# The last output projection with seven block products (Strassen) for each pair of token tiles in place of eight

## The chip, the core and the metric

The kernel runs on one core of one Trainium2 chip. A core has five engines that work side by side, each on its own queue in order: TensorE (PE in the profile, its weight loads PEld), VectorE (DVE), ScalarE (ACT), GpSimd (POOL) and SyncE (SP), which here only issues DMAs. ACT issues DMAs too. TensorE writes its results to PSUM, eight banks of 512 f32 columns; the other data lie in SBUF, 128 partitions wide. The metric is the device time of one execution in microseconds, lower is better. The kernel before takes 1339.58 us (median of 3 runs, 1339.54 to 1339.79).

## The reference

The program is one step of a two-layer backbone: a gated linear attention (GLA) layer, then a grouped-query attention layer, on 256 context tokens and 1024 latent tokens with 1024 features. What the change touches is the last line of the second layer:

```python
out_p = (attend_blocks(qp, kp, vp) * jax.nn.silu(gp)) @ att_w_out[i]
...
out_s = (attend_blocks(qs, keys, vals) * jax.nn.silu(gs)) @ att_w_out[i]
xp = xp + gt_p * out_p
xs = xs + gt_s * out_s
```

So 1280 rows of 1024 gated values are multiplied by a 1024 x 1024 matrix, scaled column by column with a gate vector and added to the residual. All of it is f32.

## The kernel before

**Precision.** TensorE is fed with f16. Each f32 matrix is scaled by a power of two and split into a high part (the f16 rounding) and a low part (the rest, again f16). A product is three matmuls: high x high, high x low, low x high (`mm3`, L120, which is why most matmuls have line 125). The high part is made by ACT, the low part by VectorE with a scalar-tensor-tensor operation that reads the f32 source and the high part. The scale comes from a maximum (VectorE), a small matmul that spreads it over the partitions (`pow2`, L79, the matmul is L84) and a chain of small VectorE operations.

**Stages.** After the start (the modulation vectors, the first normalisation) comes the GLA loop (`gla`, L642) with 50 slots, one for a head and a token tile. In a slot TensorE does projections, the scan's matmuls and whatever `filler` adds: the later weights are loaded, scaled and split here in jobs. `split_ahead` (L189) does that for the second layer's weights, 256 columns a job: load into a `wst` buffer (there are two), four maxima, the scale, four high parts (L203), four low parts (L204), and four DMAs to DRAM. `AHEAD` names the slots; the four jobs for `att_w_out` (names `o0`, `o1`) are the last ones, at slots 25 to 31. The scan's state passes through GpSimd (L571), as do a sum of two masked matrices (L537) and other small operations.

After the GLA's output projection the attention (`attention`, L1057) runs ten steps of four heads. For each head and pair of token tiles: scores (L974) into an S tile of three PSUM banks (there are two S tiles), the maximum (L977), the exponential (L982), the split of the probabilities by GpSimd (L1003) and VectorE (L1004), and a transposing DMA into `PT` (L1005). Two heads later `values` (L1018) multiplies `PT` with the values, 30 matmuls of 256 columns, and writes the gated result to `og2_d` in DRAM. `gateT` (L1008) makes the gate from `hT_hi` and `hT_lo`, the normalised activations; the last `gateT` is the last reader of these two tiles. In steps 6 and 9 the split output weights come back from DRAM into the `wtile` places 2 and 1 (`wload`, with the DMAs handed out one a head through `later`).

**The last projection.** Token tiles are taken in pairs in the order `OUT = (1, 0, 2, 3, 4)`. `out2_load` (L1103) brings the pair's 256 rows back, transposed, into `wst`; `out2_prep` (L1108) takes two maxima (L1113), the scale, two high parts (L1120) and two low parts (L1121), each of 1024 columns. `out_tile` (L1126) does one token tile: `residual` (L715) multiplies it with 512 columns of the weights at a time, 24 matmuls for a bank of an S tile, then VectorE scales (L723) and adds the residual row (L724) and ACT issues the store (L726). The first pair's operands are made in the attention's last step, in the place of the rotary table (`ropet`), and its first token tile stands ahead of the last two `values`; the rest is in `att_out` (L1135). The last tile is cut into 512, 256 and 256 columns.

**Order.** The program is written for a scheduler that tracks which instruction needs which, simulates the engines' times when the kernel is built and fixes the order on each engine by that; `issue_after` holds a block behind a given instruction. The order on the chip is therefore near to the program's order, but not the same: loads are issued where their buffer comes free, and two token tiles' matmuls alternate.

## Time and profile before

| | |
|---|---|
| median of the runs | 1339.58 us |
| the profiled execution, first to last instruction | 1339.8 us |
| granted TensorE clock, mean | 0.980 |
| TensorE busy | 1240.6 us (93%) |
| VectorE busy | 928.7 us (69%) |
| ScalarE busy | 662.8 us (49%) |
| GpSimd busy | 402.0 us (30%) |
| first matmul of the last projection | 1220.48 us |
| last matmul of it | issued and done by 1336.04 us |

The page gives busy time by engine over the whole span. The windows give the same for a stretch. The chain that ended last is followed back from the last instruction, at each step to what released it; in order of time it reads as "start, duration, what". A group row reads: line, engine, operation, output <- inputs, shapes, count | total busy us, mean ns of one | idle time ahead of it and what ended it. A row of one line's view gives minimum, median and maximum instead of a mean. All in all 22669 instructions are recorded.

### The profile page before, as it was taken

To read this page: it belongs to the slowest core of one execution; us is meant where nothing else is said; L and a number is where in the kernel's file an instruction comes from. 1 tells how busy PE (TensorE), PEld (TensorE's weight loads), DVE (VectorE), ACT (ScalarE), POOL (GpSimd) and SP (SyncE) were. 2 spreads that over 40 slices of the span, in tenths; PEclk is the share of its full clock that TensorE was granted. 3 is DMA by queue.
4 is the path that set the end of the run, shared out by engine and by line. 5 is a ranking of instruction groups with operands and counts; after the bars stand their busy time and mean duration, and the time that the engine had idled before them with its cause. 6 is when DMAs were issued, how large, how long until landed. Compare 5 with 4: busy or idle time off the path is not lost. (4 is left out here: it accounts for less than half of the span.)

```text
span 1339.8 us, 22669 instructions
## 1 busy us (share of the span) xinstructions
PE 1240.6 (93%) x8150; PEld 808.5 (60%) x8150; DVE 928.7 (69%) x2138; ACT 662.8 (49%) x1661; POOL 402.0 (30%) x623
## 2 busy tenths in 40 slices
PE   4789999999999999698899998999988998989998
PEld 2357765655555556475677656767665766766444
DVE  1876868886868688756564567878567687877552
ACT  2565546655646566533333455555556565553110
POOL 1232213322322133401222435544333343523000
PEclk9899999999999999898999999999989999999999
DMA  9612455544545532357552278877938748788532
GB/s 306 226 63 93 145 181 182 160 150 155 185 134 170 174 114 83 96 166 227 142 150 101 66 201 140 144 138 131 197 72 169 147 80 150 173 150 195 179 134 79
DMA packets 344770, 199.15 MB, mean 149 GB/s; under 512 B 229406, under 2 KB 331534, under 8 KB 343376
## 3 DMA queue, kind: packets, MB, share of 16 engines
q1 hardware_dynamic: 297024, 159.67, 47.5%
q10 hardware_dynamic: 47312, 37.25, 8.8%
q8 instruction: 64, 1.05, 0.3%
q0 software_dynamic: 320, 0.77, 0.2%
q14 instruction: 50, 0.41, 0.1%
HBM read 104.31 MB, written 37.24 MB: 106 GB/s over the span
## 5 line engine op out<-in xcount | busy, mean ns | idle before, releaser
L125 PEld LDWEIGHTS <-hT_hi 128*128 128x128 f16 x1440 | 142.5, 99 | 105.3 <-issue 9.6
L125 PE MATMUL mm<-whi,hT_hi 128*128 128x512 f16 (+1 forms) x560 | 196.6, 351 | 7.9 <-ACT gx L471 7.8
L125 PE MATMUL mm<-wlo,hT_hi 128*128 128x512 f16 (+1 forms) x560 | 196.4, 351 | 0.0
L125 PE MATMUL mm<-whi,hT_lo 128*128 128x512 f16 (+1 forms) x560 | 196.3, 351 | 0.0
L125 PEld LDWEIGHTS <-whi 128*128 128x128 f16 x1368 | 134.2, 98 | 76.2 <-issue 9.2
L1003 POOL TENSOR_SCALAR phl<-p,srec 128x1280 f16<-128x1280 f32 (+1 forms) x80 | 106.4, 1330 | 198.6 <-DVE srec L998 106.6
L125 PE MATMUL mm<-hT_hi,whi 128*128 128x256 f16 (+1 forms) x512 | 153.3, 302 | 4.3 <-POOL hT_hi L349 2.9
L125 PE MATMUL mm<-hT_lo,whi 128*128 128x256 f16 (+1 forms) x512 | 153.8, 301 | 0.2 <-DVE hT_lo L350 0.2
L125 PE MATMUL mm<-hT_hi,wlo 128*128 128x256 f16 (+1 forms) x512 | 153.8, 301 | 0.0
L1004 DVE SCALAR_TENSOR_TENSOR phl<-p,srec,phl 128x1280 f16<-128x1280 f32 (+1 forms) x80 | 107.5, 1344 | 54.0 <-POOL phl L1003 53.9
L125 PE MATMUL mm<-PT,vh 128*128 128x256 f16 x672 | 118.4, 281 | 20.2 <-DMA PT<-phl 13.5
L974 PE MATMUL S<-kT,wst 128*128 128x512 f16 (+1 forms) x624 | 122.1, 338 | 3.6 <-ACT p L982 3.6
L982 ACT ACTIVATE p<-S,snb,sexp 128x1280 f32<-128x1280 f32 (+1 forms) x80 | 99.6, 1245 | 19.4 <-DVE srec L998 9.7
L977 DVE TENSOR_REDUCE smx<-S 128x1 f32<-128x1280 f32 (+1 forms) x80 | 101.5, 1270 | 11.0 <-PE S L974 10.9
L125 PEld LDWEIGHTS <-hT_lo 128*128 128x128 f16 x720 | 71.2, 99 | 49.4 <-DVE hT_lo L350 0.5
L125 PE MATMUL mm<-PT,vl 128*128 128x256 f16 x336 | 94.5, 281 | 0.0
L974 PEld LDWEIGHTS <-wst 128*128 128x128 f16 x624 | 61.0, 98 | 55.1 <-issue 4.2
L125 PEld LDWEIGHTS <-wlo 128*128 128x128 f16 x720 | 70.6, 98 | 37.3 <-issue 1.6
L125 PEld LDWEIGHTS <-vh 128*128 128x128 f16 x672 | 66.9, 101 | 33.7 <-issue 15.0
L147 DVE TENSOR_REDUCE wmx<-wst 128x1 f32<-128x512 f32 x104 | 64.5, 676 | 23.7 <-DMA wst<-in_gla_w_in 9.8
L979 ACT ACTIVATE snb<-smx,nsexp 128x1 f32<-128x1 f32 x80 | 23.4, 293 | 110.7 <-DVE smx L977 105.0
L125 PE MATMUL y<-whi,ogT 128*128 128x256 f16 (+1 forms) x336 | 75.8, 316 | 2.6 <-DVE p2s L96 1.0
(335 smaller groups left out, 2705.2 us busy)
## 6 DMA issues: line engine op xcount, KB each, us to landing
wada<-in_w_ada SPq DMA_DIRECT2D x16, 1024.0 KB, 5.0
wst<-in_gla_w_in SPq DMA_DIRECT2D x12, 1024.0 KB, 5.7
wst<-in_att_w_in SPq DMA_DIRECT2D x10, 1024.0 KB, 8.4
xr<-x_d SPq DMA_DIRECT2D x11, 512.0 KB, 3.3
og_d<-gx ACTq DMA_DIRECT2D x40, 128.0 KB, 1.8
og_d<-og ACTq DMA_DIRECT2D x40, 128.0 KB, 3.0
wst<-og_d SPq DMA_DIRECT2D x5, 1024.0 KB
out<-xr ACTq DMA_DIRECT2D x17, 256.0 KB, 2.0
```

What stands on the lines that cost most here:

```text
L125: self.nc.tensor.matmul(out, a, b, start=k == 0 and j == 0, stop=k == n - 1 and j == 2)
L147: nc.vector.tensor_reduce(mx[:, j : j + 1], st[:, 2 * j : 2 * j + 2, :], AX.XY, ALU.max, apply_absolute_value=True)
L974: nc.tensor.matmul(S[:, a : a + n], x, y, start=m == 0, stop=m == 2)
L977: last = nc.vector.tensor_reduce(mx, S, AX.X, ALU.max).ins
L979: nc.scalar.activation(nb, mx, AF.Copy, scale=self.nsexp)
L982: nc.scalar.activation(p, S, AF.Exp, scale=self.sexp, bias=nb, accum_out=den)
L1003: nc.gpsimd.tensor_scalar(hi, p, r, 2.0 ** 14, ALU.mult, ALU.mult)
L1004: nc.vector.scalar_tensor_tensor(lo, p, r2, hi, ALU.mult, ALU.subtract)
```

## The change

The 2 x 2 block form of the product is used in Winograd's version of Strassen's method. For a pair of token tiles the left matrix is cut in two by tokens (128 each) and in two by the inner dimension (512 each), the weights in two by the inner dimension and in two by columns. Eight block products of 12 matmuls (4 inner steps x 3) become seven, of these operands: left a11, S2, S1, S3, a12 - S2 and so on (sums of quarters), right B11, T2, T1, T3, B22, T4, B21. The sums are formed in f32, then split into high and low parts; the scales leave room for a factor of four.

- *Weights.* `split_ahead` no longer handles `att_w_out`. `split_products` does, a generator with four parts that run in two slots, four times (slots 25 to 33): GpSimd scales four quarters in place, forms four differences and three of the low parts, ACT makes seven high parts, VectorE four low parts; seven DMAs go to `win_d`. Four of the seven weight blocks are loaded where `o0` and `o1` were; the other three go into `hT_hi` and `hT_lo` when these are free.
- *Operands.* `sums` and `sums_rest` make seven operands of 512 columns a pair (`cut`: high part on ACT, low part on VectorE), with four sums on GpSimd. Rows of odd pairs are loaded into a second place (`og1`, in `hT_lo`), so two loads can be on the way.
- *Products.* `pair_start` does the first four products, `pair_end` the other three, of which each accumulates onto an earlier product in its bank. Two copies by ACT, four additions by VectorE and one by GpSimd combine them. `store` scales (VectorE), adds the residual (two of four on VectorE, two on GpSimd; in the last pair three on VectorE) and issues the DMA. The fourth bank is the one of the pair's scale matmul (for the first pair, a bank of the other S tile). The last product of the last pair is cut into two halves of 256 columns.
- The first pair's `pair_start` stands ahead of the last two `values`, `pair_end` behind them.

```diff
+    def split_products(self, b, st):
+        s, inv = self.scale(st)
...
+        for x in (b11, b22, b12, b21):
+            nc.gpsimd.tensor_scalar(x, x, s4, 1.0, ALU.mult, ALU.mult)
+        def put(m, x):
...
+            nc.scalar.copy(hi, x)
+            (nc.gpsimd if m in (B11, B21, T4) else nc.vector).tensor_tensor(lo, x, hi, ALU.subtract)
+            nc.scalar.dma_start(self.win_d[:, m, :, b], t[0][:, (t[1] - 1) % 2])
+        sub = lambda o, x, y: nc.gpsimd.tensor_tensor(o, x, y, ALU.subtract)
+        put(B11, b11)
+        put(B22, b22)
+        sub(b11, b12, b11)
+        sub(b12, b22, b12)
+        sub(b22, b22, b11)
+        yield
+        put(T1, b11)
+        put(B21, b21)
+        yield
+        put(T3, b12)
+        put(T2, b22)
+        yield
+        sub(b21, b21, b22)
+        put(T4, b21)
+        yield
...
         self.rest()
+        self.out2_load(OUT[1], self.og1)
+        for j, (t, m) in enumerate(((self.hT_hi, 2), (self.hT_lo, 1))):
...
+                for part in range(2):
+                    self.nc.sync.dma_start(w[:, part], self.win_d[:, len(wo), part])
...
+        self.fold_gate(1, self.win_inv, gt)
...
+        pair = self.pair_start(OUT[0], ops, wo, x, scale, [tmp[:, 512 * j : 512 * j + 512] for j in range(3)])
...
+        self.sums_rest(row, ops, scale)
         for t in pend:
             self.values(*t, g.pop(t[0]))
+        self.pair_end(*pair)
...
+    def cut(self, x, s, to):
+        nc.scalar.activation(to[:, 0], x, AF.Copy, scale=s)
+        nc.vector.scalar_tensor_tensor(to[:, 1], x, s, to[:, 0], ALU.mult, ALU.subtract)
...
+    def sums(self, og, to, late=True):
...
+        ps = self.bank("mm") if late else None
+        s, inv = self.pow2(m, ps=ps)
+        a11, a12, a21, a22 = self.quarters(og)
+        g = nc.gpsimd.tensor_tensor
+        g(a21, a21, a22, ALU.add)
+        self.cut(a11, s, to[0])
+        g(a11, a21, a11, ALU.subtract)
+        self.cut(a21, s, to[2])
+        self.cut(a11, s, to[1])
+        g(a21, a22, a11, ALU.subtract)
+        self.cut(a21, s, to[3])
+        return s, inv, ps
+    def sums_rest(self, og, to, scale):
+        a11, a12, a21, a22 = self.quarters(og)
+        self.nc.gpsimd.tensor_tensor(a11, a12, a11, ALU.subtract)
+        self.cut(a11, scale[0], to[4])
+        self.cut(a22, scale[0], to[5])
+        self.cut(a12, scale[0], to[6])
+    def product(self, ps, x, w, start=True, b=0, n=4):
+        for k in range(4):
+            for j, (u, v) in enumerate(((0, 0), (0, 1), (1, 0))):
+                self.nc.tensor.matmul(
+                    ps[:, P * b : P * (b + n)], x[:, u, k], w[:, v, b : b + n, k],
...
+    def pair_start(self, c, ops, w, x, scale, tmp):
...
+        self.product(ps[0], ops[0], w[B11])
+        nc.scalar.copy(t1, ps[0])
+        self.product(ps[1], ops[1], w[T2])
+        self.product(ps[2], ops[2], w[T1])
+        nc.scalar.copy(t3, ps[2])
+        nc.vector.tensor_tensor(t2, ps[1], t1, ALU.add)
+        self.product(ps[3], ops[3], w[T3])
+        nc.gpsimd.tensor_tensor(t3, t3, t2, ALU.add)
+        nc.vector.tensor_tensor(t3, ps[3], t3, ALU.add)
+    def pair_end(self, c, ops, w, x, inv, u, v, ps, last=False):
...
+        store(1, 1, v)
+        self.product(ps[2], ops[4], w[B22], start=False)
+        nc.vector.tensor_tensor(ps[2], ps[2], u, ALU.add)
+        store(0, 1, ps[2], add=nc.vector)
+        self.product(ps[3], ops[5], w[T4], start=False)
+        nc.vector.tensor_tensor(u, ps[3], u, ALU.add)
+        store(1, 0, u, add=nc.vector if last else nc.gpsimd)
+        for b, n in ((0, 2), (2, 2)) if last else ((0, 4),):
+            self.product(ps[0], ops[6], w[B21], False, b, n)
+            store(0, 0, ps[0], b, n, nc.vector)
     def att_out(self, wo):
...
+        now = prep(1, self.og1)
+        og = get(2)
+        for n in range(1, 5):
+            later = get(n + 2)
+            nxt = prep(n + 1, og) if n < 4 else None
...
+            self.pair_end(*self.pair_start(c, ops, wo, x, scale, tmp), last=n == 4)
+            now, og = nxt, later
...
         def filler(slot):
+            n, m = divmod(slot - PRODUCTS, 2)
+            if 0 <= n <= 4 and (n, m) != (4, 1):
+                if m == 0:
+                    if n:
+                        next(rounds[0])
+                    if n < 4:
+                        rounds[:] = [k.split_products(n, k.stage_out(n))]
+                        k.jobs.append((next, rounds[0]))
+                else:
+                    next(rounds[0])
+                    k.jobs.append((next, rounds[0]))
```

More of the change, by code (lines that the diff above doesn't have):

```diff
@@ L44 @@
 OUT = (1, 0, 2, 3, 4)
+PRODUCTS = 25
+B11, T2, T1, T3, B22, T4, B21 = range(7)
 G_SCALE = 32.0
@@ L139, in stage, with stage_out @@
         self.nc.sync.dma_start(st, ap.rearrange("(k p) n -> p k n", p=P))
+        return st
+    def stage_out(self, b):
+        st = self.t(self.wst, [P, KT, 256], F32, "wst")
+        src = self.I["att_w_out"][0].rearrange("(k p) (x b n) -> p k x b n", p=P, x=2, b=4)
+        for x in range(2):
+            self.nc.sync.dma_start(st[:, :, P * x : P * x + P], src[:, :, x, b])
         return st
@@ L1091, in attention @@
                     first = self.ropet.rearrange("p a b d -> p (a b d)").bitcast(F16)
-                    first = first.rearrange("p (j h t) -> p j h t", j=2, h=AH)
+                    first = first.rearrange("p (m a k t) -> p m a k t", m=4, a=2, k=4)
                     with self.tc.issue_after(self.last):
-                        self.prep = self.out2_prep(row, (first[:, 0], first[:, 1]))
+                        ops = [first[:, m] for m in range(4)]
+                        scale = self.sums(row, ops, False)
@@ L1111, in out2_prep, with quarters @@
+    def quarters(self, og):
+        v = og.rearrange("p (x k) (r t) -> p r x k t", x=2, r=2)
+        return [v[:, r, x] for r in range(2) for x in range(2)]
+    def sums(self, og, to, late=True):
+        nc = self.nc
         mx = self.t(self.small, [P, 2], F32, "wmx")
@@ L1264, in emit @@
             cols += [(f"q{b}", W[:, 512 * b : 512 * b + 512]), (f"g{b}", W[:, g0 + 512 * b : g0 + 512 * b + 512])]
[L1265 removed]
         cols = [(n, j, w[:, 256 * j : 256 * j + 256]) for n, w in cols for j in range(2)]
         queue = [(0, b) for b in (8, 9, 10, 11)] + [(1, b) for b in (4, 5, 6, 7, 0, 1, 2, 3, 8, 9, 10, 11)]
[L1268 removed]
+        wo, part, prep, held, rounds = [], [], [], [], []
         def filler(slot):
```

117 lines of the change are left out of this document (75 added, 42 removed).

## The prediction

> **What bounds the kernel now.** I read the page's first part, then the chain that ended last, then the groups by line, then the windows around the two places that the diff touches. The page names one engine:
>
> ```profile
> PE 1240.6 (93%) x8150; PEld 808.5 (60%) x8150; DVE 928.7 (69%) x2138; ACT 662.8 (49%) x1661; POOL 402.0 (30%) x623
> ```
>
> The chain, in order of time, says how TensorE spends the last stage, in which the output projection runs. The first row is from the timeline: the first matmul of that stage.
>
> ```profile
> 1220.48 0.38 PE L125 MATMUL S<-whi,ropet 128*128 128x512 f16 x1
> ```
> ```profile
> 1230.95 0.70 DVE p L724
> 1231.65 0.04 issue
> ...
> 1237.04 3.38 PE mm L125 x31
> ...
> 1275.61 0.22 PE mm L84 x2
> ...
> 1291.60 36.27 PE S L125 x168
> 1327.87 0.03 issue
> 1327.89 0.77 DVE S L723
> 1328.66 0.02 issue
> 1328.69 0.70 DVE xr L724
> 1329.39 0.04 issue
> 1329.43 2.79 PE S L125 x24
> ...
> 1333.25 2.79 PE S L125 x24
> ...
> 1336.07 0.50 DVE S L723
> 1336.60 0.42 DVE xr L724
> ```
>
> One 128x512 matmul costs 36.27/168 = 0.216 us, one of 256 columns 2.79/24 = 0.116 us in this stage and 3.38/31 = 0.109 us in `values`. From 1220.48 to the end of the last matmul, 1336.04, are 115.6 us. The work in it is the equivalent of 480 x 0.216 = 103.6, two `values` of 30 matmuls (6.5) and four scale matmul pairs (0.9): 111.0. So 4.6 us are idle. What I read there: TensorE waits for VectorE's add on one bank of an S tile before it writes the next bank of the same S tile (1329.43 follows 1329.39, 1231.70 follows 1231.65). Where two token tiles alternate this is covered; in the last tile it isn't. After the last matmul 1339.8 - 1336.04 = 3.8 us are left (scaling, addition, store).
>
> **The change part by part.** The sum is made against the profiled span, 1339.8; the median of the runs, 1339.58, is 0.2 lower.
>
> *Removed on TensorE.* 5 pairs x 12 matmuls = 60 x 0.216 = -12.9 us, all of it on the path. The moving operand becomes four pieces of 128 columns, 512 elements apart; the decay matmul already reads two such pieces and costs what contiguous 256 columns cost (273 in the hT row further down), so I add nothing:
>
> ```profile
> L484 PE MATMUL z<-wa,r 98*128 98x256 f16 x40 | 11.0, 274 | 0.2 <-DVE g L493 0.2
> ```
>
> The 4.6 us idle also goes out of the sum and idle of the new order comes in. Base: 420 x 0.216 + 6.5 + 0.9 = 98.1; 1220.5 + 98.1 + 3.8 = 1322.4 without any wait.
>
> *(a) End of the last pair.* The last product is halved within one bank. After product six VectorE adds, scales and adds again (0.689 + 0.756 + 0.689, rows below, 2.2 with gaps); the first half takes 12 x 0.116 = 1.4, and its scaling and addition (0.50 + 0.42) come only after those. The second half starts 3.2 after product six: 1.8 us idle. The wait between banks of one S tile returns between products one and two (ACT's copy, 0.72): 0.9. Product four has its own bank and could cover it; between pairs the next pair covers it. Sum +2.7, bounds 1.8 to 1.8 + 5 x 0.9 = 6.3.
>
> *(b) VectorE and GpSimd in the pairs.*
>
> ```profile
> L204 DVE SCALAR_TENSOR_TENSOR split<-wst,p2s,split 128x512 f16<-128x512 f32 x56 | 40.8, 760 | 7.2 <-ACT split L203 7.1
> L203 ACT ACTIVATE split<-wst,p2s 128x512 f16<-128x512 f32 x56 | 37.4, 720 | 24.6 <-DVE p2s L96 18.1 <-DMA w_g<-split 3.1 <-DMA w_q<-split 1.9
> L723 DVE SCALAR_TENSOR_TENSOR S<-S,p2i,wst 128x512 f32<-128x512 f32 x19 | 14.4, 756 | 35.8 <-PE S L125 35.8
> L724 DVE TENSOR_TENSOR xr<-S,xr 128x512 f32<-128x512 f32 x17 | 11.7, 689 | 1.1 <-DMA xr<-x_d 0.8
> L1113 DVE TENSOR_REDUCE wmx<-wst 128x1 f32<-128x1024 f32 x10 | 11.7, 1210 | 5.8 <-DMA wst<-og_d 5.8
> L1121 DVE SCALAR_TENSOR_TENSOR wlo<-wst,p2s,whi 128x1024 f16<-128x1024 f32 x8 | 10.1, 1280 | 5.4 <-ACT whi L1120 5.4
> L88 DVE TENSOR_REDUCE p2m<-o 128x1 f32<-128x128 f32 x32 | 9.1, 283 | 3.1 <-PE o L84 2.8
> L96 DVE TENSOR_SCALAR p2s<-p2e 128x1 int32<-128x1 int32 x47 | 7.1, 150 | 1.0
> ```
>
> VectorE per pair, before: two maxima 2.4, scale chain 0.28 + 5 x 0.15 = 1.0, two low parts 2.6, four scalings and additions 5.8: 11.8 of 96 x 0.216 + 0.2 = 20.9. After: 2.4 + 1.0 + seven low parts of 512 (7 x 0.76 = 5.3) + four sums of products (2.8) + four scalings (3.0) + two additions (1.4) = 15.9 of 84 x 0.216 + 0.2 = 18.3, so 87%. ACT has 9 x 0.72 = 6.5 and is no bound. GpSimd, idle in this stage, gets seven 128x512 tensor-tensor operations. No row has that size; the shortest of two sizes give the slope:
>
> ```profile
> L835 POOL TENSOR_TENSOR rope<-hx,ropet x160: 307/320/1566, 647.5 to 1172.2; 128x64 f32<-128x64 f32 x160
> ```
> ```profile
> L537 POOL TENSOR_TENSOR at<-am x40: 450/534/867, 112.1 to 540.1; 128x128 f32<-128x128 f32 x40
> ```
>
> (450 - 307)/64 = 2.2 ns per element, so 1.3 us for 512 and 9.2 us per pair. The maxima of these rows are the warning, and the next three rows explain them:
>
> ```profile
> 1206.97 2.54 POOL L1003 TENSOR_SCALAR phl<-p,srec 128x1280 f16<-128x1280 f32 x1 [3.70 <-DVE srec L998]
> ```
> ```profile
> 1207.11 1.28 DVE L1121 SCALAR_TENSOR_TENSOR ropet<-wst,p2s,ropet 128x1024 f16<-128x1024 f32 x1
> ...
> 1208.37 2.21 DVE L1121 SCALAR_TENSOR_TENSOR ropet<-wst,p2s,ropet 128x1024 f16<-128x1024 f32 x1
> ```
>
> A low part with both inputs in SBUF runs first while GpSimd's operation takes 2.54; the second low part then takes 2.21 in place of 1.28 and ends 1.07 after GpSimd. They exclude each other. [...] Nine VectorE operations of a pair have two SBUF inputs (seven low parts, two scalings): 6.8 of 15.9. If GpSimd's work falls beside the other 9.1, VectorE stays at 15.9; if every GpSimd operation holds it up, 15.9 + 9.2 = 25.1. At 43% of 9.2, 4.0 at most and half of that when the meeting is in mid-operation: 17.9 to 19.9, about 18.9, against 18.3. Three pairs carry both a pair's sums and the next one's operands: +2.0, bounds 0 and 3 x 6.8 = 20.
>
> *(c) Weights that come late.* Three of the seven weight blocks (3 MB) and 1 MB of values go into `hT`, which is read until 1220.4.
>
> ```profile
> L125 PE MATMUL mm<-hT_hi,wlo x55: 272/273/273, 1149.8 to 1220.4; 128*128 128x256 f16 x55
> ```
> ```profile
> 1229.60 3.06 SPq L1005 DMA_TRANSPOSE PT<-phl  x1
> ...
> 1245.43 0.32 SPq L1105 DMA_DIRECT2D wst<-og_d  x1
> ```
> ```profile
> 1250.72 2.35 DVE L1113 TENSOR_REDUCE wmx<-wst 128x1 f32<-128x1024 f32 x2 [0.43 <-DMA wst<-og_d]
> ```
>
> A load of 1 MB takes 1250.72 - 1245.43 = 5.3 us. The last block is wanted at 1220.5 + 72 x 0.216 + 6.5 = 1242.6; four loads issued at 1220.5 are there by 1241.7. If SyncE's queue puts them behind the last transpose (1232.7) they end at 1253.9: 11.3 late. Transposes also queue behind them, and `values` wait for those. I take +1.5, bounds 0 and 11.3. The gate rows and residual rows have buffers that are free earlier.
>
> *(d) The weight sums in the GLA loop (slots 25 to 33, 387 to 501 us).* Same loads, maxima and number of low parts on VectorE; ACT's copies rise from 4 to 7 a round, 12 x 0.72 = 8.7. GpSimd gets 4 scalings, 4 differences and 3 low parts a round: 4 x 0.86 + 7 x 1.3 = 12.5, four rounds 50 us.
>
> ```profile
> L349 POOL TENSOR_SCALAR hT_hi<-h 128x512 f16<-128x512 f32 x16 | 13.6, 856 | 35.8 <-ACT h L348 35.6
> ```
> ```profile
> core 0: us, PE busy (x) PEld busy (x) DVE busy (x) ACT busy (x) POOL busy (x), PEclk, DMA share, GB/s
> 387.00:501.00 114.00, 111.83 (x641) 64.40 (x639) 89.05 (x240) 67.72 (x181) 29.74 (x53) 1.00 0.48 153
> 501.00:552.00 51.00, 43.83 (x263) 31.10 (x261) 44.42 (x136) 31.38 (x89) 20.89 (x36) 0.98 0.19 63
> 760.00:900.00 140.00, 132.68 (x922) 90.41 (x921) 109.02 (x203) 80.02 (x207) 70.42 (x95) 0.99 0.74 146
> ```
>
> [...] Nearest rows: with GpSimd at 50% and VectorE at 78% TensorE is at 94.8%, which here is 114 x (0.981 - 0.948) = 3.8; with VectorE at 87% it is at 85.9%, 13.9. GpSimd will be at 70%, so I take +4, bounds 0 and 13.9 (a gain is excluded: TensorE's work there stays the same).
>
> *(e) The attention's end.* The first pair's operands take VectorE 4 x 0.76 in place of 2 x 1.28 and GpSimd three operations (3.9) in front of a softmax part (1206.97): +1, bounds 0 and 3.9. The other weight loads there are as many and as large as before.
>
> Sum: 1322.4 + 2.7 + 2.0 + 1.5 + 4 + 1 = 1333.6 in the span, 1333.4 as a median.
>
> **The rivals.**
>
> - *Everything is covered.* Only (a) is left: 1322.4 + 2.7 = 1325.1. For it: TensorE's 98% in the GLA window. [...]
> - *The GLA loop pays (slower side).* GpSimd's rounds stand ahead of the scan's operations on an engine that works in order, VectorE is blocked, and TensorE falls to 85.9%: 1333.4 + 9.9 = 1343.3. It decides from a loss of 4 + 6.2 = 10.2 us on. Against it: GpSimd idles 84 of 114 us there.
> [...]
> - *Weights behind the last transpose.* 1333.4 + 9.8 = 1343.2, less where TensorE has `values` to do.
>
> **How the numbers follow.** Forecast 0.44, all covered 0.18, GLA loop 0.16, port 0.14, late weights 0.08. The rivals on the slow side reach down through no change in part. A measurement of this kernel can tell 0.2%, 2.7 us, from no change: faster is below 1336.9, slower above 1342.3. Faster 0.44 + 0.18 = 0.62; within 0.13 (parts of the last three); slower 0.25. The range 1324 to 1346 leaves out the all-covered case with product four in the gap (0.04) and the port above half its bound.
>
> **What would show it.** Right: `product` at 420 matmuls of about 0.216; the first of them at 1220 plus what (d) and (e) cost; low parts between 0.76 and 2 us; the GLA window at 95% PE. (c) is wrong if TensorE waits for a DMA of the weight tiles before product five; (b) if TensorE waits for VectorE before a pair's first product; (d) if the first `product` starts before 1221 or after 1230. The forecast fails if GpSimd or VectorE is the engine of the last chain.

## The result, and the profile after

The changed kernel takes 1358.8 us (median of 4 runs, 1357.36 to 1362.09) against 1339.68 us for the kernel before (4 runs, 1339.54 to 1347.72): ratio 1.0123, 95% interval 1.0085 to 1.0161. The forecast was 1333.4, the range 1324 to 1346. The change makes the kernel slower, and the result lies above the range.

The first part of the page of the changed kernel, busy time by engine, and its chain by engine and line:

```profile
PE 1240.0 (91%) x8078; PEld 802.3 (59%) x8078; DVE 976.6 (72%) x2178; ACT 685.1 (50%) x1708; POOL 501.8 (37%) x701
...
PE 4%; DVE 3%; DMA 1%; POOL 1%; issue 0%; ACT 0%; SPq 0%; POOLq 0%; DVEq 0%
```

TensorE has fewer instructions (8078, before 8150) and the same busy time (1240.6 before): what the missing matmuls gave came back as slower ones (the mean granted clock is 0.972, before 0.980). VectorE has 48 us more, GpSimd 100. The last chain was nearly all TensorE before (its row of the page is below); now a part as long as TensorE's runs through other engines.

```profile
PE 8%; DVE 0%; issue 0%
```

Five points of time say where the 17.2 us between the two spans (1357.0 - 1339.8) arise. They are starts, in us, from the views of single tiles: the first matmul of the GLA's output projection (this stage is called gla_out below), the first scores, the last read of `hT`, and the end. Experiments stand in the same table, because most of them are read by it.

| kernel | gla_out | scores | last `hT` | end | end - last `hT` |
|---|---|---|---|---|---|
| before | 616.5 | 776.0 | 1220.4 | 1339.8 | 119.4 |
| changed | 634.8 | 791.9 | 1239.1 | 1357.0 | 117.9 |
| e1 rounds as before | 618.2 | 772.8 | 1216.3 | 1336.0 | 119.7 |
| e2 no GpSimd | 620.5 | 775.6 | 1217.1 | 1335.9 | 118.8 |
| e3 one job | 638.8 | 796.3 | 1239.5 | 1358.8 | 119.3 |
| e4 order | 639.3 | 797.2 | 1240.7 | 1358.0 | 117.3 |
| e5 fold, early scale | 639.6 | 793.8 | 1240.2 | 1362.4 | 122.2 |
| e6 VectorE alone, no late loads | 631.7 | 788.9 | 1229.1 | 1346.5 | 117.4 |
| e7 memsets, both | 627.1 | 785.4 | 1228.5 | 1341.3 | 112.8 |
| e8 GpSimd beside | 634.7 | 788.7 | 1236.6 | 1348.4 | 111.8 |
| e9 rounds moved | 611.7 | 813.6 | 1264.4 | 1376.3 | 111.9 |
| e10 memsets beside, not held | 618.1 | 774.8 | 1216.4 | 1330.7 | 114.3 |
| e11 early operands | 634.4 | 791.8 | 1236.3 | 1349.4 | 113.1 |
| e12 half of e8 | 625.5 | 783.1 | 1222.7 | 1334.9 | 112.2 |
| e13 memsets in place | 619.9 | 775.9 | 1219.2 | 1330.2 | 111.0 |
| e14 moved, spread | 613.2 | 788.8 | 1235.7 | 1348.0 | 112.3 |
| e15 / e17 moved, in place (one program) | 616.7 / 618.4 | 788.0 / 785.1 | 1230.5 / 1225.9 | 1343.2 / 1338.5 | 112.7 / 112.6 |
| e16 moved, later | 617.5 | 790.2 | 1240.4 | 1352.3 | 111.9 |
| e18 product order | 611.6 | 778.9 | 1225.4 | 1340.1 | 114.7 |

How far a number can be trusted: every row is one execution. The GLA loop is one and the same in the changed kernel, e4 and e11, which give 634.8, 639.3 and 634.4, and in e15, e17 and e18, which give 616.7, 618.4 and 611.6; e15 and e17 are one program, whose stage from gla_out to scores took 171.3 and 166.7. So differences below some 7 us in one cell say nothing. Whole executions of the kernel before scatter as well: those timed beside the experiments took between 1336.3 and 1358.7 us. The end of the last projection is steadier. From the start of the last `values` matmul to the end of the kernel take 94.1 to 95.1 us in the four kernels that share this stage (changed, e1, e2, e3), 91.9 in e4, 86.5 to 88.0 in the nine kernels where pair one's operands are made early (e8, e9, e11 to e17), and 89.6 in e18.

The loss is made up of +18.3 us up to gla_out, -2.4 from there to the scores, +2.8 in the attention, and only -1.5 in the last projection, which should have brought the gain. One of the 35 products of the changed kernel (12 matmuls, 2.6 us) starts at 1233.8, ahead of the last read of `hT`. So 2.6 of the attention's 2.8 us belong to the last projection, which is then 1.1 us longer than before, and not shorter.

**The GLA loop.** The windows of busy time from slot 25 to slot 34 (before, 387 to 501: the row is in the prediction) for the changed kernel:

```profile
388.10:523.20 135.10, 121.97 (x651) 66.89 (x650) 105.18 (x246) 73.64 (x196) 81.86 (x99) 0.95 0.44 144
```

135.1 us in place of 114.0. GpSimd has 52 us more, as forecast (50). VectorE has 16 us more busy time for nearly as many operations (246, before 240): its operations got longer. Of the 21.1 us, 11.0 are TensorE's idle time and 10.1 its longer busy time; the granted clock of 0.95 in place of 1.00 can make up to 0.05 x 135.1 = 6.8 of these. Two groups of VectorE in this window before the change, the same two behind it, and two pairs of neighbours from the changed kernel's timeline:

```profile
L494 DVE SCALAR_TENSOR_TENSOR g<-ls,g 128x256 f32<-128x256 f32 x10 | 4.4, 438 | 0.0
...
L227 DVE SCALAR_TENSOR_TENSOR ls<-gx,ls 128x256 f32<-128x256 f32 x10 | 4.3, 432 | 1.5 <-ACT ls L226 1.5
```

```profile
L545 DVE SCALAR_TENSOR_TENSOR g<-ls,g 128x256 f32<-128x256 f32 x10 | 6.8, 679 | 0.0
...
L278 DVE SCALAR_TENSOR_TENSOR ls<-gx,ls 128x256 f32<-128x256 f32 x10 | 6.0, 605 | 1.4 <-ACT ls L277 1.3
```
```profile
409.08 1.33 POOL L243 TENSOR_TENSOR wst<-wst 128x512 f32<-128x512 f32 x1
...
416.74 1.27 POOL L243 TENSOR_TENSOR wst<-wst 128x512 f32<-128x512 f32 x1
```
```profile
409.21 1.49 DVE L545 SCALAR_TENSOR_TENSOR g<-ls,g 128x256 f32<-128x256 f32 x1
...
416.85 1.71 DVE L198 SCALAR_TENSOR_TENSOR wlo<-wst,p2s,whi 128x512 f16<-128x512 f32 x1 [0.17 <-ACT whi L197]
```

An operation of 128x256 with two inputs in SBUF takes 0.438 us in the mean before the change, and again in e13 below. Here it starts 0.13 us after GpSimd's difference, ends 0.3 us after it, and takes 1.49. In the second pair a low part, 0.75 us in the mean before the change, starts 0.11 us after GpSimd's difference, ends 0.55 after it and takes 1.71.

TensorE then stands, and pays twice. One wait of the changed kernel's timeline and the matmuls behind it:

```profile
487.81 0.22 PE L559 MATMUL cs<-cum,glo 128*128 128x130 f16 x1
492.32 0.59 PE L130 MATMUL mm<-whi,hT_hi 128*128 128x512 f16 x1 [4.29 <-DVE s L347]
492.70 0.63 PE L130 MATMUL mm<-wlo,hT_hi 128*128 128x512 f16 x1
493.12 0.63 PE L130 MATMUL mm<-whi,hT_lo 128*128 128x512 f16 x1
```

After 4.29 us of nothing the matmuls follow each other at 0.43 us in place of 0.216, until 497.4, at a granted clock of 0.50.

**The last projection.** The groups hold 420 matmuls of 512 columns' worth, 0.216 us apart, as forecast. One product (2.6 us) is done before 1239.1, so without waits the rest would end the kernel at 1239.1 + 98.1 - 2.6 + 3.8 = 1338.4; 18.6 us are lost. TensorE's timeline from the first pair's last product on, and VectorE's where it waits for the load:

```profile
1263.00 2.83 PE L1222 MATMUL S<-hT_lo,whi 128*128 128x512 f16 x12
1265.67 0.38 PE L89 MATMUL mm<-ident,wm 128*128 128x128 f32 x2
1270.43 0.80 PE L89 MATMUL mm<-ident,wm 128*128 128x128 f32 x2 [4.37 <-DVE wm L1198]
1272.67 4.83 PE L1222 MATMUL S<-whi,ops 128*128 128x512 f16 x14 [1.44 <-ACT ops L1183]
1278.13 2.33 PE L1222 MATMUL S<-whi,ops 128*128 128x512 f16 x10 [0.63 <-DVE ops L1184]
...
1282.80 2.33 PE L1222 MATMUL S<-wlo,ops 128*128 128x512 f16 x10 [1.48 <-DVE ops L1184]
```
```profile
1267.05 2.35 DVE L1194 TENSOR_REDUCE wmx<-wst 128x1 f32<-128x1024 f32 x2 [3.36 <-DMA wst<-og_d]
...
1269.97 0.28 DVE L93 TENSOR_REDUCE p2m<-mm 128x1 f32<-128x128 f32 x1
```

Between the first pair and the second, called pair zero and pair one, TensorE waits 7.9 us in four pieces and 3.7 more in the 25 us ahead of it, and a part of the matmuls here runs at a lower clock (4.83 us for 14, 3.19 when they are 0.216 apart; the granted clock from 1272.6 to 1277.5 is 0.65). From 1290 to 1343 it is busy nearly without a gap; 2.6 us of waits stand in the last two pairs.

### The profile page after: what moved, and what is told of

It is laid out like the page before. It is cut to its first block, busy times and chain, and to the rows that moved or that the text cites. A ratio compares the mean times of both kernels' runs of the same rounds, so it can differ in the third digit from the quotient of the medians.

```text
span 1357.0 us, 22758 instructions
## 1 busy us (share of the span) xinstructions
PE 1240.0 (91%) x8078; PEld 802.3 (59%) x8078; DVE 976.6 (72%) x2178; ACT 685.1 (50%) x1708; POOL 501.8 (37%) x701
## 5 line engine op out<-in xcount | busy, mean ns | idle before, releaser
L1057 POOL TENSOR_SCALAR phl<-p,srec 128x1280 f16<-128x1280 f32 (+1 forms) x80 | 103.6, 1294 | 196.8 <-DVE srec L1052 101.5
L130 PEld LDWEIGHTS <-whi 128*128 128x128 f16 x1096 | 107.6, 98 | 47.4 <-issue 7.8
L1036 ACT ACTIVATE p<-S,snb,sexp 128x1280 f32<-128x1280 f32 (+1 forms) x80 | 99.5, 1244 | 25.3 <-DVE srec L1052 10.1
L1033 ACT ACTIVATE snb<-smx,nsexp 128x1 f32<-128x1 f32 x80 | 23.5, 293 | 112.8 <-DVE smx L1031 107.5
L400 POOL TENSOR_SCALAR hT_hi<-h 128x256 f16<-128x256 f32 (+1 forms) x64 | 37.1, 585 | 104.6 <-ACT h L399 103.5
```

The source lines that it names most:

```text
L130: self.nc.tensor.matmul(out, a, b, start=k == 0 and j == 0, stop=k == n - 1 and j == 2)
L400: nc.gpsimd.tensor_scalar(hi, h, 1.0, 1.0, ALU.mult, ALU.mult)
L1033: nc.scalar.activation(nb, mx, AF.Copy, scale=self.nsexp)
L1036: nc.scalar.activation(p, S, AF.Exp, scale=self.sexp, bias=nb, accum_out=den)
L1057: nc.gpsimd.tensor_scalar(hi, p, r, 2.0 ** 14, ALU.mult, ALU.mult)
```

## The experiments

### e1 to e4: where does each loss come from

Theories for the GLA loop: A, GpSimd's work, with what it does to VectorE's operations beside it ("port" in the author's texts stands for this, in the prediction's rows a low part of 2.21 in place of 1.28 us; what lies behind it no run shows); B, the `wst` buffers, held through two slots, make later loads late; C, ACT's further high parts. For the last projection: D, VectorE's order, in which pair two's maxima (waiting for a load, above) stand ahead of pair one's scale; E, the loads themselves. e1 has neither GpSimd's sums nor buffers held for long nor further high parts, so A, B and C all expect the time of before from it (a span of 1338 to 1341 us).

```diff
# e1: as before the change; one job a round
...
+    nc.scalar.activation(hi, x, AF.Copy, scale=s)
+    nc.vector.scalar_tensor_tensor(lo, x, s, hi, ALU.mult, ALU.subtract)
...
# e2: nothing on GpSimd
-    nc.gpsimd.tensor_scalar(x, x, s4, 1.0, ALU.mult, ALU.mult)
...
+    sub = lambda o, x, y: None
# e3: the four parts of a round in one job
+    k.jobs.append((list, k.split_products(n, k.stage_out(n))))
# e4
+    with self.tc.issue_after(self.tail):
         nxt = prep(n + 1, og) if n < 4 else None
```

> The weight rounds of the GLA loop work as before the change (one job per 256 columns: one scale, four high parts on ACT, four low parts on VectorE straight from the staged block, nothing on GpSimd, staging buffer given back in the same slot); four plain quarters are stored, three of them twice, so all seven blocks are written but T1 to T4 hold no sums. The last stage is that of the changed kernel. [...]

> The changed kernel without GpSimd's work in the weight rounds: the four scalings, four differences and three low parts of each round are left out (ACT applies the scale; for the three blocks whose low part GpSimd made, the high part is stored twice; T1 to T4 hold no sums). Buffers are held through two slots and ACT makes seven high parts as in the changed kernel. Theory A: slot 34 starts at 501 to 507, the GLA loss of 18.6 us falls below 6, span 1339 to 1345. Theory B: the loads of slot 32's weights are still late (issued after 475, 457.8 before), slot 34 starts after 511, span above 1349. Theory C: the same as B, with ACT as the engine waited for in slots 26 to 33.

> The changed kernel with the four parts of a weight round put into one job, so that the staging buffer comes free about one slot earlier; every instruction is kept. Theory A: the same GpSimd and VectorE work in a denser burst, GLA loss 18.6 or more (slot 34 at 522 to 530), span 1355 to 1364. Theory B: the loss falls below 10 (slot 34 before 512, the load for slot 32 issued before 470), span below 1349. Theory C: as A.

> The changed kernel with one order of VectorE changed in the last stage: the operands of pair n+1 (maxima, scale, low parts) are queued behind the last low part of pair n, so pair two's maxima, which waited 3.36 us for a load, no longer stand ahead of pair one's scale. Theory D (VectorE's order makes the 13 us lost between 1240 and 1290): pair one's scale is read at 1266 instead of 1270, TensorE's 4.37 us wait at its scale matmul falls below 1, the last stage ends 4 to 6 us earlier, span 1351 to 1353. Rival E (the loads behind the transposes set the pace, VectorE's order only fills the gap): the wait moves to TensorE's products of pair one, span 1356 to 1358. The GLA loop stays at its 18.6 us loss under both.

Measured, up to gla_out: e1 618.2 and e2 620.5, 1.7 and 4.0 above before, less than the scatter; e3 638.8, no better than the change. So GpSimd's work in the rounds, with all that waits for it, is the whole loss, and C and B have no part that can be seen: e2 has ACT's seven high parts and holds the buffers through two slots; e3, which frees them earlier, gains nothing. The last projection: e4 gains 0.6 us in the table (4 to 6 expected by D). In place of the waits at 1270.43 and 1272.67 there is one of 2.85 us for pair one's first high part, and a low part is waited for 2.21. From the last `values` on e4 is 2.2 us shorter than the changed kernel, but ahead of them TensorE waits 2.56 us for a transpose (1.40 in the changed kernel). So VectorE's order is a part of it, at most half of what D expected.

### e5 to e7: less GpSimd, no GpSimd, GpSimd that reads nothing

```diff
# e5, e6: scale inside the split, all low parts on VectorE (e6: the differences too)
+    nc.scalar.activation(hi, x, AF.Copy, scale=s4)
+    nc.vector.scalar_tensor_tensor(lo, x, s4, hi, ALU.mult, ALU.subtract)
# e5, e7: e4's order, and pair one's scale ahead of the second values
+    self.scale1 = self.maxima(self.og1, self.S2[1][:, 0:512])
# e6, e7: no late loads
+    wo.append(wo[len(wo) - 4])
# e7: GpSimd's operations become memsets of the same tiles
+    nc.gpsimd.memset(x, 0.25)
```

> Two edits in two stages, read apart by the first matmul of the gla_out stage (616.5 before, 634.8 changed) and by the time from the last read of hT to the end (119.4 before, 117.9 changed). First edit: the weight rounds scale inside ACT's copy and VectorE's low part, all seven low parts on VectorE, GpSimd keeps only the four differences: 16 x 1.3 = 20 us of GpSimd in place of 51, VectorE 12 x 0.76 = 9 us more. Theory A, GpSimd's time beside VectorE is what costs: 18.3 x 20/51 = 7 us of loss stay, first gla_out matmul at 622 to 626. Rival F, VectorE's own time decides: the loss stays above 12 us, 629 or later. Second edit: the scale of pair one (maxima, its matmul, its chain) is taken in front of the second values, and a pair's operands are queued behind those of the pair before. Theory G (TensorE runs out of operands between pair zero and pair one because pair one's scale matmul stands behind pair zero's last product): 117.9 falls to 111 to 114. Rival E (loads set the pace): 116 or more.

> Two edits in two stages, read apart as above. First edit: as the fold of the run before, and the four differences on VectorE too, so that GpSimd has nothing in the weight rounds: VectorE gets 12 x 0.76 + 16 x 0.69 = 20 us more in a window where it was idle 25 of 114 us. Theory A: no stretching of VectorE's other operations, first gla_out matmul at 617 to 624. Rival F: VectorE is now the bound, 628 or later. Second edit: the three late weight blocks (3 MB) are not loaded in the last stage; products five to seven read three resident blocks in their place (other values, same matmuls). Rival E (the loads delay the transposes and the next pair's values): TensorE's waits for transposes and for pair one's operands fall from 10 us to 4, the time from the last hT read to the end falls from 117.9 to 111 to 113. Theory G: the transposes' waits (2 us) go, pair one's stay, 115 to 117.

> Two edits in two stages, read apart as above. First edit: GpSimd's eleven operations of a weight round are eleven memsets of the same tiles (the blocks then hold constants), so GpSimd is busy in the same places of its queue but reads nothing of SBUF. Theory A in its port form: VectorE's 128x256 operations with two SBUF inputs are back at 0.43 to 0.46 us (0.55 to 0.68 in the changed kernel) and the first gla_out matmul is at 622 or before. Rival H, GpSimd's queue (the scan's operations stand behind the round's): 628 or later with VectorE's operations at their old length. If a memset takes less than half of the 1.26 us the test is weak on H. Second edit: the early scale and order of the run before the last together with the three blocks not loaded: if G and E each hold for a part, 117.9 falls to 107 to 110; if one of them alone does, the number is that of the run with that edit.

The first edits: theory A missed in e5 and e6, and both came where rival F, VectorE's own time, had put them. e5 with 22 us of GpSimd in place of 51 is no faster (639.6): VectorE has 12 low parts more, and beside the differences its operations of 128x256 are still longer (0.557 us in the mean of the group `g`, 0.438 in e6). e6 without GpSimd still loses 15 us (631.7). VectorE is busy for 102.6 of 129.1 us there, so its time alone isn't the bound: TensorE waits 6.4 us for ACT's `v`, whose copies stand in ACT's queue behind the rounds' high parts, and these wait 7.2 us for VectorE's scale and 15.8 for the stores that empty the split buffer. e7 loses 10.6 us (627.1), between what the port form of A (622 or before) and rival H, GpSimd's queue (628 or later), had asked. Its VectorE operations are at their old length (0.414 us in the group `g`, 0.417 in `ls`), and yet TensorE waits for the gate's copy by ACT:

```profile
PE mm L130 <- ACT gx L525: 5.6, 5, 2.8
```

So there can be two prices: reads of GpSimd beside VectorE, and a chain of scale or sum, high part, low part and store, each of which can wait for the one before it (in e6 VectorE's low parts wait 12.1 us for ACT's high parts). How much of the changed kernel's loss the chain makes isn't shown by e7 (its memsets take 0.525 us, less than half of a difference).

The second edits, with theory G (TensorE runs out of operands of pair one) against E: without the late loads 117.4 (e6), no gain. With the scale early and e4's order (e5) 122.2, worse. Two rows first, the end of pair one's scale chain on VectorE and the next operation of ACT:

```profile
1260.93 0.14 DVE L103 TENSOR_SCALAR p2i<-p2e 128x1 int32<-128x1 int32 x1
```
```profile
1268.59 0.72 ACT L1183 ACTIVATE ops<-hT_lo,p2s 128x512 f16<-128x512 f32 x1 [14.86 <-PE mm L130]
```

The scale is there at 1261.1, and pair one's first high part starts at 1268.6, when the last `values` are done. Its tile lies in the pool that is opened after the attention's pools are closed, and the place is read until then. So an earlier scale can't bring the operands forward. But TensorE doesn't wait for them here, as its rows show:

```profile
1262.26 0.59 PE L130 MATMUL mm<-PT,vh 128*128 128x256 f16 x2 [3.58 <-DMA PT<-phl]
...
1268.39 2.75 PE L1226 MATMUL S<-hT_hi,whi 128*128 128x512 f16 x12
1270.98 2.75 PE L1226 MATMUL S<-hT_lo,whi 128*128 128x512 f16 x12
1273.57 2.75 PE L1226 MATMUL S<-whi,ops 128*128 128x512 f16 x12
```

In e5 product six of pair zero (at 1268.39) came to stand behind the last `values`; in the changed kernel it is ahead of them. So TensorE has nothing to do until their transpose is there (3.58 us, 0.63 in the changed kernel), the `values` behind the wait are slow (0.59 us for two, 0.38 elsewhere), and then products six and seven cover pair one's first operands. That the memory holds the operands back is shown; that this costs time isn't. E has a part: with the same edits and no late loads (e7) the time is 112.8, for without them the last `values` are done 20 us after the last `hT` read, with them 28 (e5; 2.6 of the difference are one product more ahead of them). The loads delay the transposes, and these the values: in e5 the last transpose, issued behind the first loads, takes 8.64 us in SyncE's queue, before the change 3.06.

### e8 and e9: GpSimd's reads alone; the rounds elsewhere

```diff
# e8: rounds as in e1, and beside them, 4 and 7 a round
+    one = lambda: nc.gpsimd.tensor_scalar(self.scr, u, inv, 1.0, ALU.mult, ALU.mult)
+    two = lambda: nc.gpsimd.tensor_tensor(self.scr, u, v, ALU.subtract)
# e8, e9 and later: pair one's first four operands in free columns of hT
+    free = [t.rearrange("p k n -> p (k n)")[:, 8192 + 1024 * j : 9216 + 1024 * j] for t in (self.hT_hi, self.hT_lo) for j in range(2)]
...
+    self.pair1 = ops1, self.sums(self.og1, ops1)
     self.values(*v2, g.pop(v2[0]))
# e9: in gla_out, once or twice a token tile
+    next(rounds, 0)
```

> Two edits in two stages, read apart by the first matmul of the gla_out stage (616.5 before, 634.8 changed, 618.2 with the rounds as before) and by the time from the last read of hT to the end (117.9 changed). First edit: the weight rounds as before the change, and beside them, in the places of the changed kernel, GpSimd's four scalings and seven two-input operations of each round on a piece of hT that nobody writes, into a scratch that nobody reads: GpSimd's time and its reads without the chain of sums that ACT and VectorE wait for (T1 to T4 hold no sums). Port theory: VectorE's 128x256 operations with two SBUF inputs take 0.52 to 0.68 us as in the changed kernel, first gla_out matmul at 626 to 635. Chain theory (the loss comes from high parts waiting for sums in ACT's queue): 618 to 622 in spite of longer VectorE operations. Both in part: 622 to 626. Second edit: pair one's scale and first four operands go into columns of hT that are free from the last hT read on, and are made in front of the second values, so they don't wait for the memory of the last softmax tile, which the run with the early scale showed them waiting for (ACT idle 14.86 us until the values were done). Theory G (operands of pair one late): TensorE has no wait of over 1 us between product seven of pair zero and product four of pair one, 117.9 falls to 110 to 113. Rival E (loads and transposes): 115 or more.

> The changed kernel with the four weight rounds moved, as they are, from the GLA loop to the gla_out stage (token tiles three to nine), where VectorE is busy 26 of 40 us and GpSimd 9 of 40, and with the tail's edit of the run before. If the GLA loss comes from too little slack beside TensorE in that window: first gla_out matmul at 612 to 618 (634.8 changed); the gla_out stage, 157.1 us from its first matmul to the first scores in the changed kernel and 159.5 before, gets 2 to 6 us longer; with the tail at 110 to 113 the time is 1328 to 1338. If the rounds cost the same wherever they stand: the stage gets 14 us or more longer, and the time is 1344 to 1352.

e8 has the whole loss, 634.7, though nobody waits for GpSimd's results: GpSimd's time and its reads are enough, without the chain. The last projection fell to 111.8, as theory G has it: in the 25 us behind the last `values` TensorE waits 0.84 and 1.58 us, both for ACT's copy between two banks of an S tile. e9 is a miss: the loop is free (611.7), but the stage takes 201.9 us in place of 157.1, ratio 1.0212 (1.0184 to 1.0240). In the views of waits VectorE stands for the load that its maxima want, and ACT for the split buffer's stores:

```profile
DVE wmx L159 <- DMA wst<-in_att_w_out: 13.6, 4, 6.2
```
```profile
ACT split L245 <- DMA win_d<-split: 21.1, 10, 5.5
```

### e10 to e13: reading or standing in line

```diff
# e10: nothing holds the memsets in their slots; e13 does
+    one = lambda: [nc.gpsimd.memset(self.scr, 0.0) for _ in range(2)]
+    two = lambda: [nc.gpsimd.memset(self.scr, 0.0) for _ in range(3)]
# e13
+    nc.gpsimd.tensor_scalar(self.scr[:, 0:4], u[:, 0:4], inv, 1.0, ALU.mult, ALU.mult)
# e11: the changed kernel with pair one's operands early (as in e8)
# e12: e8 with five of eleven operations
```

> Two edits in two stages. First edit: as the run with GpSimd's operations alone (634.7 for the first gla_out matmul, 618.2 without them), but each one-input operation is two memsets of the same scratch and each two-input operation three (0.525 us each, some 61 us in all against 53.8 us): GpSimd is as long busy in the same places of its queue and reads nothing of SBUF. Port theory: VectorE's 128x256 operations with two SBUF inputs are at 0.41 to 0.46 us, first gla_out matmul at 618 to 622. Queue theory (the scan's operations stand behind the round's): 628 or later with VectorE's operations at their old length. Second edit: pair one's operands made early (111.8 us from the last hT read to the end) and the three late weight blocks not loaded, products five to seven reading three resident blocks. If the late loads still cost, the wait for transposes (2.2 us) and the time fall to 108 to 110; if not, 111 to 112.

> The changed kernel with pair one's scale and first four operands made early in free columns of hT, nothing else. The tail falls from 117.9 to 111.8 as in the run before; the GLA loop stays. 1358.8 - 6 = 1352 to 1354 against 1339.7 before: still slower than before, ratio 1.008 to 1.011 by the medians on record. If the ratio is at or below 1.002, the GLA loop's loss isn't steady from run to run.

> As the run with GpSimd's operations alone, with five in place of eleven operations a round (24 us of GpSimd in place of 54); the tail with pair one's operands early. If the loss goes with GpSimd's reading time, 16.5 us x 24/54 = 7 us stay: first gla_out matmul at 624 to 627. If there is a threshold (the slack beside TensorE takes the first part), 618 to 621. If a few meetings at bad places make it, 630 or later.

> As the run with GpSimd's operations alone (11 a round, 54 us; first gla_out matmul at 634.7, 618.2 without them), with memsets of the scratch in their place (8 for the four one-input operations, 21 for the seven others, 0.525 us each, 61 us in all), and each round's memsets tied behind the round's scale by one operation of four columns, so that they stand in the same slots; in the run before with memsets nothing held them there and they ran at 105 to 192 us. Port theory: GpSimd as busy as there, VectorE's operations of 128x256 at 0.41 to 0.46 us, first gla_out matmul at 617 to 622. Queue theory: 628 or later. In between: both, in the proportion that the number gives. The tail has pair one's operands early: 111 to 113 us.

e10 says nothing on the queue: its memsets ran at 105 to 192 us. e13 is the pair to e8. The windows from slot 25 to slot 34, e8 first, then e13, each with a group of VectorE:

```profile
389.30:518.90 129.60, 116.74 (x643) 65.09 (x642) 110.84 (x240) 67.97 (x183) 83.89 (x98) 0.97 0.49 160
```
```profile
L268 DVE SCALAR_TENSOR_TENSOR ls<-gx,ls 128x256 f32<-128x256 f32 x10 | 6.8, 685 | 0.7 <-ACT ls L267 0.7
```
```profile
389.60:507.50 117.90, 114.21 (x654) 65.64 (x652) 88.61 (x242) 69.20 (x184) 89.98 (x175) 1.00 0.55 176
```
```profile
L271 DVE SCALAR_TENSOR_TENSOR ls<-gx,ls 128x256 f32<-128x256 f32 x10 | 4.4, 438 | 0.6 <-ACT ls L270 0.6
```

GpSimd is busier in e13 (90.0 against 83.9 us) and in the same places, and VectorE is at 88.6 against 110.8, TensorE's idle at 3.7 against 12.9, gla_out at 619.9 against 634.7. Standing in line costs 1.7 us by these cells (619.9 - 618.2), less than the scatter; reading costs the rest. Beside GpSimd's reads the group of VectorE above takes 0.685 us (e8), beside its memsets, which only write, 0.438 (e13). e12 gives the dose: 24 us of reading cost 625.5 - 618.2 = 7.3, 54 us cost 16.5: about 0.30 us for each us. No free part can be seen, though with single executions that scatter by up to 7 us a small one isn't excluded.

e11, the change with nothing but early operands, is at 1353.84 against 1344.24, ratio 1.0075 (1.0047 to 1.0102): part of the loss is undone, as expected. e10's last stage, early operands without late loads, is 114.3: no gain from their absence can be seen there either.

### e14 to e18: can the change be made to pay

```diff
# e14: a block is loaded one round ahead, a round in seven steps, scale and low parts as in e5
+    st = self.t(self.pst, [P, KT, 256], F32, "pst") if b % 2 == 0 else self.t(self.wst, ...)
# e15, e17: three products written into used-up quarters
+    put(T3, b12, b11)
+    put(T2, b22, b12)
...
+    put(T4, b21, b22)
# e16: three steps a token tile, seven more at the end
# e18: e15, and in all pairs but the first
+    self.product(ps[3], ops[3], w[T3])
     self.product(ps[1], ops[1], w[T2])
```

> The changed kernel with the weight rounds in the gla_out stage again, this time spread: each round in seven small steps over token tiles three to nine, its block loaded a whole round ahead into one of two buffers, the scale inside ACT's copy and VectorE's low part, all low parts on VectorE, only the four differences a round (22 us) on GpSimd, the scale's matmul in another PSUM bank than the key tiles'; and the tail with pair one's operands early. In the first run with the rounds moved the stage took 201.9 us in place of 157.1 from its first gla_out matmul to the first scores, with VectorE waiting 13.6 us at the head of its queue for loads and ACT 21.1 us for stores. If those waits made the loss: 158 to 170 us, first gla_out matmul at 611 to 614, span 1328 to 1340. If the sums' reads and the chain cost as in the GLA loop: 172 to 180 us, span 1342 to 1350. If the stage can't take any more work: above 185, span above 1355.

> As the run with the rounds spread over the gla_out stage (stage 175.6 us, 157.1 in the changed kernel; ACT waited 24.9 us for the stores out of the two split buffers), but three of a round's seven products write their high and low parts into quarters of the staged block that are used up, so that only four go through the split buffers. If ACT's waits for stores, at the head of its queue, are the rest of the stage's loss: these waits fall below 10 us, the stage to 160 to 168 us, span 1332 to 1341. If they only filled time in which ACT had nothing to do: the stage stays at 172 or more, span 1345 or more.

> The run before (stage 171.3 us) with the rounds' steps at a slower pace, three a token tile and the last seven among the last key tiles and the first queries: in that run VectorE was busy 36 and 32 of 40 us in 640 to 720 and 24 and 21 of 40 us in 720 to 800. If VectorE's crowding in the first half makes the rest: the stage falls to 160 to 167 us, the time to 1333 to 1340, at or below the kernel before. If the sums' price is the same anywhere in the stage: 170 or more, 1343 or more.

> The kernel of the run with used-up quarters as split buffers (rounds in the gla_out stage, pair one's operands early), timed against the kernel before: 1344.96 against 1340.68 there, in one run each. If that difference is steady the ratio is 1.002 to 1.006, faster than the change as it was made (1.0123) and still not faster than before. Below 1.000 would mean that the single run was an unlucky one.

> The kernel of the run before (rounds in the gla_out stage, pair one's operands early; ratio 0.998) with one more edit: in all pairs but the first the fourth product, which has a PSUM bank of its own, is done second, so that ACT's copy of the first product no longer stands between two banks of one S tile (TensorE waited 0.69 and 1.58 us there). If this is the prediction's term (a): the two waits go, the tail falls from 112.6 to 110 or 111, ratio 0.995 to 0.998. If the wait only moves to the next product on that tile: 112 to 113 and a ratio as before.

With the waits for loads and stores made smaller the stage goes from 201.9 (e9) to 175.6 (e14) and 171.3 or 166.7 (e15, e17), against 157.1 in the changed kernel. So most of e9's loss went with an earlier load, smaller steps and less work on GpSimd (22 us in place of 51); e14 made these edits together, and which of them brought how much isn't shown. In e15 ACT's waits for the split buffers' stores fall from 24.9 us to 15.0 (below 10 was expected). Some 10 to 14 us stay, and a slower pace doesn't take them away (e16, 172.7; ratio 1.0081, 1.0047 to 1.0115). What they are wasn't parted further. e17 is at 0.9984 of the kernel before (0.9951 to 1.0017), below the 1.002 to 1.006 that were expected: the change then costs nothing and brings nothing that can be told. e18 missed its aim: TensorE's waits of 0.68 and 1.57 us on ACT's copy are still there, a third of 1.36 comes in, and from the last `values` on it takes 89.6 us where e15 and e17 take 88.0 and 87.3; the ratio is the same (0.9986, 0.9954 to 1.0017). No kernel with all seven products' sums was found that is faster than the one before.

## Why the prediction was wrong

The forecast for the span was 1333.6; it came to 1357.0, 23.4 more. By stage: term (d) 18.3 in place of 4 (+14.3), the last projection 117.9 in place of 98.1 + 3.8 + 2.7 + 2.0 + 1.5 = 108.1 (+9.8), the gla_out stage -2.4, the attention +2.8 in place of +1; the 0.1 that is left is rounding. With the product that ran ahead of the last `hT` read put where it belongs, the last projection's miss is 12.4 and the attention's -0.8.

- *The base* (420 matmuls at 0.216, pieces of 128 columns at no extra price) is right.
- *(a)* is right in size: 0.30, 0.75 and 1.59 us are lost in the last two pairs, 2.6 in place of 2.7. The 1.59 is the wait at the cut last product (1.8 forecast). The other two aren't where the 0.9 was put, between products one and two for ACT's copy, but ahead of product five for VectorE's addition; that they add up to nearly as much is luck.
- *(b)* is right in kind, with low parts between 0.74 and 1.76 us; five scalings with an input in PSUM that ran beside GpSimd in the changed kernel kept their 0.76 us. It is too high where it was put: from 1290 on, where a pair's sums and the next one's operands meet, TensorE loses next to nothing. What it loses to VectorE's low parts (0.63 and 1.48 us) lies at pair one. "Port" in the chances and the range is the case that GpSimd's operations, by holding VectorE up (a pair at up to 25.1 us), limit the last stage; no run shows that.
- *(c)* didn't happen. TensorE waits for no weight tile before product five, and without the late loads the change gains 0.5 us (e6). The loads do delay the transposes, as the prediction said they could (8.64 in place of 3.06 us for the last one in e5); it cost where TensorE had no product left ahead of the last `values` (122.2 in e5, 112.8 in e7), and nothing that can be seen elsewhere (e6, e10).
- *(d)* is the step that failed first. GpSimd's 50 us were right, and that it holds VectorE up was named; but the price was taken from a window in another stage (GpSimd 50%, VectorE 78%, TensorE 94.8%) as if it went by busy shares, with 13.9 as a bound. The bound doesn't bound: it comes from operations that are there in that stage, not from 51 us of reading beside VectorE's operations with two SBUF inputs. What the runs showed in its place: 18.3 us of loss, which goes with the time that GpSimd reads (e8 and e12 against e13). The prediction's own rows (a low part of 2.21 in place of 1.28 us beside an operation of GpSimd that took 2.54, its median in the kernel before being 1.36) would have shown the kind of price, as they did for the pairs. TensorE's 98%, counted in favour of "everything is covered", is the wrong way round: at 98% there is nothing left to cover with, and by e8 and e12 each us of reading costs about 0.30. The window that was to stay at 95% is at 90.3% (121.97 of 135.1 us). The rival "GLA loop pays" had the stage, the sign and the blocking, and with 1343.3 too small a price; GpSimd's place in line, its first cause, is worth 1.7 us by e13, less than the scatter.
- *(e)* can't be told: the attention's 444.4 us before and 447.2 after (444.6 without the product) lie inside the 439.6 to 450.8 of all kernels here.
- *A term that was left out*: pair one's operands. The sum went through a pair in steady state and through the end, not through the passage from the first pair, whose operands were made ahead, to the second, whose aren't. Two things hold them back: their memory (e5) and the place of their scale's matmul behind product seven, which is the later one in the changed kernel (its last `values` end at 1263.2, its product seven at 1265.8). Both taken away bring 4.8 to 6.1 us (e11, e8), and 6.8 to 7.3 from the last `values` on. VectorE's order alone (e4) brings 2.2 there, and the early scale with that order (e5) nothing in the whole stage; the memory alone wasn't tried.
- *What a measurement can tell* was put at 0.2%. The interval of the result is 0.4% to each side, and the kernel before scattered by 22 us over all its executions here.

Two figures of the sum are off by 0.1 or 0.2 (8.7 for 12 x 0.72, +2.0 for 3 x 0.6); they change nothing.

By its own tests the prediction said (d) would be wrong if the first product started after 1230: 1233.8.

## What to carry to other kernels

Work on an idle GpSimd wasn't free where VectorE was busy with operations that have two SBUF inputs (0.685 us beside its reads, 0.438 beside its memsets): price it by the time that GpSimd reads SBUF, and ask what TensorE's share is in that window; at 98%, 24 us of reading already cost 7.3 us here. Giving the work to VectorE was no way out: e6 lost 15 us. A new loop's first turn wants a working of its own: what was made ahead for turn zero, and where do turn one's inputs lie, who reads that memory last, and what stands ahead of their first instruction? Where order is fixed when the kernel is built, a change of order that helps at one wait can move other work (product six in e5), so the whole stage has to be read again after it.

## What was not expected of the hardware

TensorE's idle time cost more than itself. After 4.29 us the next 12 matmuls came at half the pace, 0.43 us apart, for 5.1 us (492.3 to 497.4, granted clock 0.50), so some 2.5 us more are lost than the wait shows; in the changed kernel's window that is part of why TensorE's busy time rose by 10 us with almost as many matmuls. The length of a wait alone doesn't decide, though: in e17 the matmuls behind a wait of 2.59 us are slow too, and in e4 those behind one of 2.85 are not. The rows are e17's and then e4's, two matmuls each, of 256 columns (0.38 us at full pace, as further down in the same kernels) and of 512 (0.59):

```profile
1232.00 0.61 PE L130 MATMUL mm<-PT,vh 128*128 128x256 f16 x2 [2.59 <-DMA PT<-phl]
...
1248.09 0.38 PE L130 MATMUL mm<-PT,vh 128*128 128x256 f16 x2 [0.48 <-DMA PT<-phl]
```
```profile
1272.10 0.60 PE L1222 MATMUL S<-whi,ops 128*128 128x512 f16 x2 [2.85 <-ACT ops L1183]
```
